# Dense attention's first three steps in a written order, two projection stores on SyncE's queue, softmax maxima apart from stored tiles, and one modulation group moved from layer 0's feed-forward part to layer 1's

## The chip, the cores and the metric

One core of one Trainium2 chip. The metric is device microseconds of one execution; the time of a kernel is the median of its runs.

## The reference, cut to what matters

Two layers (`DEPTH` = 2) over a sequence of 1024 tokens of width 1024. Each layer computes six modulation vectors from the condition c, projects the normed x once for three groups of heads, attends in three ways, projects back, and runs a gated feed-forward part:

```python
for l in range(DEPTH):
    mod = cond @ w_mod[l] + b_mod[l]
    sh_a, sc_a, gt_a, sh_f, sc_f, gt_f = [m[:, None, :] for m in split_cols(mod, (D,) * 6)]
    h = rms_norm(x, g_attn[l]) * (1 + sc_a) + sh_a
    proj = h @ w_in[l]
    ...
    ya = neighborhood_attention(...)        # 4 heads (A)
    yb = sliding_window_attention(...)      # 6 heads (B)
    yc = axial_attention(...)               # 6 heads (C), dense softmax over 1024 keys
    ...
    y = jnp.concatenate([rms_norm(ya, ga), rms_norm(yb, gb), rms_norm(yc, gc)], axis=-1)
    x = x + gt_a * (y @ w_o[l])
    h = rms_norm(x, g_ffn[l]) * (1 + sc_f) + sh_f
    gate, up = split_cols(h @ w_gu[l], (FFN_HIDDEN, FFN_HIDDEN))
    x = x + gt_f * ((jax.nn.silu(gate) * up) @ w_down[l])
return rms_norm(x, g_final)
```

## The kernel before, in words

All matmuls are float32 products made of three matmuls on split operands: an operand is cast to a high part (ACT, `CAST`) and the rest is kept as a low part (DVE, a subtraction). Each layer runs in four stages: the projection, attention, the output projection, and the feed-forward part.

**Who sets the order.** Every engine is wrapped (class `Engine`, lines 36 to 61). Where an engine is pinned (`pin(..., True)`) its instructions keep the order in which the code writes them; where it isn't, a scheduler orders them. Since the wrapper issues every instruction, all of them have line 49 in the profile, and rows are told apart by their tiles.

**The projection's end.** The loop over `oc` (line 1179) projects heads A and B in eight blocks of columns with two halves each (tile `ps_ab`, split into `qko`) and stores each to memory one turn later (`store(act)`, and a last one at line 1203: `qkd<-qko`). In block 7, `early_scores` (line 1161) computes scores, maxima and exponentials of the first two pairs of heads C, whose probabilities lie in `pr` and `wst`. Then pools are closed, and those of attention opened over their space (`y`, `att`), so that a new tile can lie where a stored tile lay and then has to wait until the store has read it.

**Attention** is one stream of 64 pairs of 128-query blocks (`stream`): 24 of heads C (`PairC`, line 1325), 16 of heads A, 24 of heads B. Step n of the loop at line 1587 works on several pairs at once. For heads C it transposes pair n (`turn`: tile `T`, four transposes for four key blocks, cast by ACT and split by DVE to `pt`), multiplies the transposed probabilities of pair n−1 with the values (`pv`), and computes pair n+3's scores (`qk`, which calls `c_scores`, line 1139: four matmuls to a bank of `sC`, of which there are two; DVE's maximum `rs`; ACT's exponential `pr` with its sum). A pair's reciprocals (DVE) and its scaling (POOL) come when both its blocks are done (`divide`, line 1155; `finish` puts them in `unfinished`). Steps with n < 0 only make pairs and their scores. On SP's queue stand, at this place, stores of v for heads A (`vAd<-vs`), tables of biases (`skA`, `skB`), loads of v (`vs<-vAd`) and later the loads of q and k for heads A and B (`qk<-qkd`).

**Modulation in pieces.** A modulation vector of 1024 columns (a group) is an accumulation over 8 blocks of rows of `w_mod`, on DVE (`acc<-wmt,condT,acc`), summed over partitions by four matmuls (`ps_mod`). Some of the groups are computed in steps spread through the projections (`mod_one`), others in the feed-forward part, where the steps are taken from a generator (`mod_stream`): one 512-column half of a block at each `next`, and at a group's end two flushes, each a cast to `acch`, a subtraction to `accl` and the two matmuls that read them. `todo` lists the groups in order; `mod_stream` goes on until a given (layer, group).

**The feed-forward part** computes seven products for each 2x2 block of columns instead of eight (`PRODUCTS`; tile `ps_w`, 12 matmuls each). DVE, POOL and ACT prepare weights (`ws`, `wpt`) and combine products (`u`, `sg`). From block `EARLY` = 7 on, each product is followed by one `next(mods_due, None)`.

Of the kernel before, what the change touches and what calls it, by code (L numbers as in the profile page):

```python
# [19 lines left out]
P = 128  # L20
# [3 lines left out]
H = 512  # L24
# [61 lines left out]
def trunk(ctx: ExitStack, tc, A, C, out):  # L86
# [5 lines left out]
    def pin(engines, on):  # L92
        for e in engines:
            e.pinned = on
# [724 lines left out]
    for l in range(2):  # L819
# [319 lines left out]
        def c_scores(h, j, c, pr, rs):  # L1139

            g = qkC[h // 3]
            s = psS.tile([P, 1024], F32, name="sC", tag="S")
            for kb in range(2):
                ks = slice(kb * 512, (kb + 1) * 512)
                for i in range(2):
                    pe.matmul(
                        s[:, ks], g[:, h % 3, j * P : (j + 1) * P], g[:, 3 + i, ks],
                        start=(i == 0), stop=(i == 1),
                    )
            dve.tensor_reduce(out=rs[:, c : c + 1], in_=s, axis=AX.X, op=ALU.max, negate=True)  # L1150
# [27 lines left out]
        for oc in range(NE, 8):  # L1178
            w = wab
            for half in range(2):  # L1180
# [9 lines left out]
                if store:  # L1190
                    store(act)
                if scored:
# [9 lines left out]
                store = ab_split(oc, half, ps, ab)  # L1202
        store(act)
        pin((pe, act, dve, pool), False)
        close(ab_cm)
# [23 lines left out]
        pad(atp, 16)  # L1229
        gss = {23: gss_tile()}  # L1230
        def pt_tile():
            return wp.tile([P, 4, 256], F32R, name="pt", tag="whl", bufs=8)
# [94 lines left out]
        class PairC(Pair):  # L1327
# [4 lines left out]

            def qk(self, c):
                pr = self.pr[c] = pr_tile()
                c_scores(self.h, 2 * self.p + c, c, pr, self.rs)
                self.finish(pr)

            def turn(self, c):
                if c == 0:
                    self.pt = [[pt_tile() for _ in range(2)] for _ in range(2)]  # L1340
                cc = slice(c * P, (c + 1) * P)
                for kb in range(2):
                    T = t_tile()
                    for i in range(4):
                        kc = kb * 4 + i
                        pe.transpose(T[:, i, :], self.pr[c][:, kc * P : (kc + 1) * P], ident)
                    split_pt(T, self.pt[kb][0][:, :, cc], self.pt[kb][1][:, :, cc])
# [253 lines left out]
        for n in range(-AHEAD - 1, N + 3):  # L1601
            ahead = AHEAD if n + AHEAD < NC else AHEAD_B
            begin = range(done, min(n + ahead + 1, N))
            if n < NC:
                for i in range(2):
                    if 0 <= n:
                        pairs[n].turn(i)
# [12 lines left out]
            else:  # L1620
# [19 lines left out]
                scored, worked = fresh, scored  # L1640
            done = max(done, min(begin.stop, made))
            while made < min(N, n + ahead + 2):
# [3 lines left out]
                made += 1  # L1646
            pin((pe, act, dve), False)
            for what in later.pop(n, []):
# [28 lines left out]
            for end, (chunks, width) in norms.items():  # L1677
                if begins[end] <= m <= end and (m - begins[end]) % 8 == 7 and (n <= NC or m >= NC):
# [9 lines left out]
                    if m == end and end < N - 1:  # L1688
# [335 lines left out]

        mods_due = mod_stream(psl, (ntp, "sq", 2, H), (1, 3))
        bs = []
# [26 lines left out]
        for q in range(NF):  # L2053
# [9 lines left out]
            for i, p in enumerate(PRODUCTS[2 if q < EARLY else 0 :]):  # L2063
# [4 lines left out]
                g_step()  # L2068
                if q >= EARLY:
                    next(mods_due, None)  # L2070
# [331 lines left out]
```

## Time and profile before

| | |
|---|---|
| median of 3 runs | 2403.49 us (2403.01 to 2408.04) |
| profiled execution | 2405.66 us |
| its span | 2403.9 us, at a mean granted TensorE clock of 0.993 |
| TensorE (PE) busy | 2337.2 us (97%) |
| VectorE (DVE) busy | 1756.9 us (73%) |
| ScalarE (ACT) busy | 1192.2 us (50%) |
| GpSimd (POOL) busy | 744.0 us (31%) |

PE is TensorE, PEld its loading of weights, SP is SyncE; a name with a q is an engine's queue of transfers. In a timeline's row stand the start and the duration in us, engine, line, operation, output<-inputs, sizes and the count of instructions drawn together; in brackets the idle time of that engine ahead of it, and whose end ended it. In a row of a stretch stand its length and each engine's busy time with its number of instructions, then the granted clock of PE (1.00 is full speed), the share of the DMA engines' time, and GB/s.

### The profile page before, as it was taken

Reading aid. Unit: us, or ns where it says so; the run is one execution under the profiler, and the core shown is the slowest. Engines: PE = TensorE matmul, PEld = TensorE weight load, DVE = VectorE, ACT = ScalarE, POOL = GpSimd, SP = SyncE. Lnnn points to the kernel's source line nnn. Section 1 sums busy time; section 2 is a strip of 40 time slices with the busy share of each in tenths; the row PEclk is TensorE's granted clock in tenths of the full one; section 3 lists DMA queues with packets and bytes.
Section 4 is the critical chain, followed back from the end, with each engine's and each line's share of the span. In section 5 each row is a group of like instructions: output and inputs, shape, how many; then the busy total and the mean of one; then the engine's idle time right before and its main releaser. Section 6 shows DMA issues by size and latency. Waiting matters only on the chain. (4 is left out here: it accounts for less than half of the span.)

```text
span 2403.9 us, 33342 instructions
## 1 busy us (share of the span) xinstructions
PE 2337.2 (97%) x11733; PEld 1954.9 (81%) x11733; DVE 1756.9 (73%) x2788; ACT 1192.2 (50%) x2250; POOL 744.0 (31%) x719
## 2 busy tenths in 40 slices
PE   8999999999999999999999999999999999999998
PEld 4788899888787887888887879988888888888886
DVE  5767898977858788587677679988797554547765
ACT  3422788944543333344543148897454334334443
POOL 1431345610244443300036114465004443430001
PEclk9999999999999999999999999999999999999999
DMA  8458316154345454586424761152534333329633
GB/s 265 138 183 278 94 62 156 45 201 129 109 137 171 155 186 152 174 265 197 155 88 123 246 215 28 44 145 74 199 103 145 114 101 106 122 88 298 213 125 110
DMA packets 305336, 356.95 MB, mean 148 GB/s; under 512 B 51964, under 2 KB 221788, under 8 KB 305168
## 3 DMA queue, kind: packets, MB, share of 16 engines
q1 hardware_dynamic: 283296, 342.07, 44.9%
q10 hardware_dynamic: 21504, 12.59, 2.0%
q8 instruction: 92, 1.51, 0.3%
q14 instruction: 76, 0.62, 0.1%
q0 software_dynamic: 368, 0.17, 0.0%
HBM read 269.79 MB, written 88.63 MB: 149 GB/s over the span
## 5 line engine op out<-in xcount | busy, mean ns | idle before, releaser
L49 PE MATMUL ps_d<-wpt 128*128 128x512 f32 x1848 | 423.8, 390 | 1.1 <-ACT wpt L49 0.7
L49 PEld LDWEIGHTS ps_d<-wpt 128*128 128x128 f32 x1848 | 345.7, 188 | 74.4 <-issue 3.0
L49 POOL TENSOR_SCALAR pr<-pr,rs 128x1024 f32<-128x1024 f32 (+2 forms) x248 | 193.0, 791 | 220.8 <-DVE rs L49 196.8
L49 POOL TENSOR_TENSOR sg<-sg,u 128x512 f32<-128x512 f32 x82 | 116.6, 1422 | 354.0 <-ACT sg L49 228.4
L49 PE MATMUL pv<-pt,vs 128*128 128x256 f32 x1088 | 175.8, 296 | 17.7 <-DVE y L49 13.4
L49 DVE TENSOR_TENSOR pt<-T,pt 128x512 fp32r<-128x512 f32 x272 | 176.9, 678 | 8.3 <-ACT pt L49 8.0
L49 ACT CAST wpt<-w 128x512 fp32r<-128x512 f32 x154 | 95.7, 621 | 174.6 <-PE ps_d L49 156.1
L49 ACT CAST pt<-T 128x512 fp32r<-128x512 f32 x272 | 151.8, 584 | 40.6 <-PE T L49 38.8
L49 ACT COPY u<-ps_w 128x512 f32<-128x512 f32 x128 | 75.1, 587 | 190.1 <-PE ps_w L49 190.1
L49 POOL TENSOR_TENSOR wpt<-ws,wpt 128x512 fp32r<-128x512 f32 x80 | 110.9, 1388 | 186.5 <-ACT wpt L49 140.3
L49 DVE TENSOR_TENSOR wpt<-w,wpt 128x512 fp32r<-128x512 f32 x154 | 108.9, 707 | 79.8 <-ACT wpt L49 77.7
L49 PEld LDWEIGHTS pv<-pt,vs 128*128 128x128 f32 x1088 | 141.7, 190 | 30.8 <-DVE y L49 26.0
L49 PE MATMUL T<-identr,pr 128*128 128x128 f32 x1176 | 161.6, 273 | 0.8 <-DVE edge L49 0.4
L49 PEld LDWEIGHTS T<-identr,pr 128*128 128x128 f32 x1176 | 137.9, 140 | 16.0 <-issue 1.3
L49 DVE SCALAR_TENSOR_TENSOR acc<-wmt,condT,acc 128x512 f32<-128x512 f32 (+1 forms) x98 | 113.9, 1172 | 44.6 <-DMA wmt<-in_w_mod_dram 44.2
L49 ACT CAST wpt<-ws 128x512 fp32r<-128x512 f32 x176 | 107.8, 622 | 60.0 <-issue 28.1
L49 DVE TENSOR_TENSOR wpt<-ws,wpt 128x512 fp32r<-128x512 f32 x96 | 82.9, 872 | 62.0 <-ACT wpt L49 61.9
L49 DVE TENSOR_TENSOR wpt<-graw,wpt 128x512 fp32r<-128x512 f32 x154 | 110.1, 715 | 17.4 <-ACT wpt L49 17.4
L49 ACT CAST wpt<-graw 128x512 fp32r<-128x512 f32 x154 | 95.0, 617 | 52.9 <-DMA graw<-gpd 48.8
L49 DVE TENSOR_REDUCE rs<-sC 128x1 f32<-128x1024 f32 x88 | 107.3, 1221 | 17.7 <-PE sC L49 12.3
L49 DVE TENSOR_TENSOR ws<-wr 128x512 f32<-128x512 f32 x88 | 78.9, 899 | 53.9 <-POOL wpt L49 50.8
L49 PE MATMUL sC<-qk 128*128 128x512 f32 x384 | 107.5, 403 | 5.8 <-ACT pr L49 5.6
(300 smaller groups left out, 5938.0 us busy)
## 6 DMA issues: line engine op xcount, KB each, us to landing
wr<-in_w_gu_dram SPq DMA_DIRECT2D x92, 512.0 KB, 4.1
gpd<-sg SPq DMA_DIRECT2D x154, 256.0 KB, 4.4
graw<-gpd SPq DMA_DIRECT2D x76, 512.0 KB, 3.5
w<-in_w_down_dram SPq DMA_DIRECT2D x110, 256.0 KB, 5.6
wmt<-in_w_mod_dram SPq DMA_DIRECT2D x48, 512.0 KB, 5.3
qk<-qkd SPq DMA_DIRECT2D x44, 512.0 KB, 7.1
wst<-in_w_o_dram SPq DMA_DIRECT2D x32, 512.0 KB, 4.1
wmt<-in_w_mod_dram SPq DMA_DIRECT2D x64, 256.0 KB, 3.6
```

What stands on the lines that cost most here:

```text
L49: ins = op(*args, **kwargs)
```

## The change

- `c_scores` is split into `c_dots` (the matmuls) and `c_exps` (the maximum and the exponential), so that they can be written apart.
- Steps n < 0 only make pairs. Step 0 is written out, and PE, ACT and DVE stay pinned from the projections through it: the first pair's transposes stand ahead of and between the third's scores, the maxima and exponentials behind the first pair's splits. In step 1 only the fifth pair's scores are computed.
- The stores of the last two halves (block 7, first half: issued one turn later, and the second half) are issued by SP instead of ACT: four transfers in each layer.
- A tile `rb` of the pool `att` is allocated earlier, so that the maxima (`rs`) come to lie elsewhere than on stored tiles.
- In layer 0's feed-forward part three groups are computed instead of four, in layer 1's one instead of none, and `next(mods_due, None)` is left out after two of the seven products.

```diff
@@ projection loop
-                    store(act)
+                    store(sp if oc == 7 and half else act)
...
-        store(act)
-        pin((pe, act, dve, pool), False)
+        store(sp)
+        pin((pool,), False)
...
         gss = {23: gss_tile()}
+        atp.tile([P, H], F32, name="rb", tag="rb", bufs=2)
@@ class PairC
+            def dots(self, c):
+                self.s = c_dots(self.h, 2 * self.p + c)
+                return lambda s=self.s: self.exps(s, c)
+
+            def exps(self, s, c):
+                pr = self.pr[c] = pr_tile()
+                c_exps(s, c, pr, self.rs)
+                self.finish(pr)
...
-            def turn(self, c):
-                if c == 0:
+            def turn(self, c, kbs=(0, 1)):
+                if c == 0 and kbs[0] == 0:
...
-                for kb in range(2):
+                for kb in kbs:
@@ the stream's loop
-            if n < NC:
+            if n < 0:
+                begin = range(done, done)
+            elif n == 0:
+                first, second, third, fourth = (pairs[i] for i in range(4))
+                first.turn(0)
+                exps = [third.dots(0)]
+                first.turn(1)
+                exps.append(third.dots(1))
+                exps[0]()
+                second.turn(0, (0,))
+                first.pv(0)
+                second.turn(0, (1,))
+                first.pv(1)
+                exps[1]()
+                begin = range(3, 4)
                 for i in range(2):
+                    exps = fourth.dots(i)
+                    if i == 0:
+                        second.turn(1)
+                    exps()
+                    while i == 0 and unfinished:
+                        unfinished.pop(0)()
+                done = 4
+                fresh = []
+            elif n < NC:
+                for i in range(2 if n > 1 else 0):
...
+                for i in range(2 if n == 1 else 0):
+                    pairs[begin[0]].qk(i)
...
-            pin((pe, act, dve), False)
+            if n >= 0:
+                pin((pe, act, dve), False)
...
-            pin((pe, act, dve), n >= NC - 1)
+            pin((pe, act, dve), n < 0 or n >= NC - 1)
@@ the feed-forward part
-        mods_due = mod_stream(psl, (ntp, "sq", 2, H), (1, 3))
+        mods_due = mod_stream(psl, (ntp, "sq", 2, H), (1 + l, 2 - 2 * l))
...
-                if q >= EARLY:
+                if q >= EARLY and i % 3 != 2:
                     next(mods_due, None)
```

Three places of the order. First, PE at the start of layer 0's attention, from the projection's last matmul on (`sC` are scores of the third and fourth pairs; `T` from `pr` transposes the first pair, `T` from `wst` the second), before:

```order
L49 MATMUL ps_ab<-hl,whi 128x512
L49 MATMUL sC<-qk 128x512 x8
L49 MATMUL T<-identr,pr 128x128 x12
L49 MATMUL pv<-pt,vs 128x256
L49 MATMUL T<-identr,pr 128x128 x4
L49 MATMUL T<-identr,wst 128x128 x4
L49 MATMUL pv<-pt,vs 128x256 x8
L49 MATMUL sC<-qk 128x512 x4
L49 MATMUL T<-identr,wst 128x128 x6
```

and after:

```order
L49 MATMUL ps_ab<-hl,whi 128x512
L49 MATMUL T<-identr,pr 128x128 x8
L49 MATMUL sC<-qk 128x512 x4
L49 MATMUL T<-identr,pr 128x128 x8
L49 MATMUL sC<-qk 128x512 x4
L49 MATMUL T<-identr,wst 128x128 x4
L49 MATMUL pv<-pt,vs 128x256 x8
L49 MATMUL T<-identr,wst 128x128 x4
L49 MATMUL pv<-pt,vs 128x256 x8
L49 MATMUL sC<-qk 128x512 x4
L49 MATMUL T<-identr,wst 128x128 x8
L49 MATMUL sC<-qk 128x512 x4
```

The first pair's transposes moved ahead of the third pair's scores, and the second's transposes and both blocks of pv stand ahead of the fourth's scores. On DVE at the same place (`qko` is the projection's last split, `pt` the splits of transposed blocks, `rs` the maxima and the reciprocals), before:

```order
L49 SCALAR_TENSOR_TENSOR qko<-ps_ab,qko 128x512
L49 TENSOR_TENSOR pt<-T,pt 128x4x128 x2
L49 TENSOR_REDUCE rs<-sC 128x1 x2
L49 TENSOR_TENSOR pt<-T,pt 128x4x128 x2
L49 TENSOR_REDUCE rs<-sC 128x1
L49 RECIPROCAL rs<-rs 128x2
```

and after:

```order
L49 SCALAR_TENSOR_TENSOR qko<-ps_ab,qko 128x512
L49 TENSOR_TENSOR pt<-T,pt 128x4x128 x4
L49 TENSOR_REDUCE rs<-sC 128x1
L49 TENSOR_TENSOR pt<-T,pt 128x4x128 x2
L49 TENSOR_REDUCE rs<-sC 128x1
L49 TENSOR_TENSOR pt<-T,pt 128x4x128 x2
L49 TENSOR_REDUCE rs<-sC 128x1
L49 RECIPROCAL rs<-rs 128x2
```

Four splits instead of two stand ahead of the first maximum, and two more ahead of the second. Third, PE in layer 0 where heads C end and heads A begin (`sA` are A's scores), before:

```order
L49 MATMUL sC<-qk 128x512 x4
L49 MATMUL T<-identr,pr 128x128 x12
L49 MATMUL sA<-qk 128x256 x2
L49 MATMUL sA<-qk 128x384 x2
L49 MATMUL pv<-pt,vs 128x256 x8
L49 MATMUL T<-identr,pr 128x128 x4
L49 MATMUL pv<-pt,vs 128x256 x8
L49 MATMUL T<-identr,pr 128x128 x8
L49 MATMUL pv<-pt,vs 128x256 x8
```

and after:

```order
L49 MATMUL sC<-qk 128x512 x4
L49 MATMUL T<-identr,pr 128x128 x12
L49 MATMUL pv<-pt,vs 128x256 x8
L49 MATMUL T<-identr,pr 128x128 x4
L49 MATMUL pv<-pt,vs 128x256 x8
L49 MATMUL T<-identr,pr 128x128 x8
L49 MATMUL pv<-pt,vs 128x256 x8
L49 MATMUL T<-identr,pr 128x128 x8
L49 MATMUL pv<-pt,vs 128x256 x6
L49 MATMUL sA<-qk 128x256 x2
L49 MATMUL sA<-qk 128x384 x2
```

The first scores of A stand 30 pv and 20 transposes later. In the feed-forward part of layer 0, PE has 24 `ps_w` matmuls between a group's two flushes in each of four groups before; after the change it has 24, 36 and 36 in three groups, and 24 in layer 1's one.

More of the change, by code (lines that the diff above doesn't have):

```diff
@@ L1139, in c_scores, with c_dots @@
         def c_scores(h, j, c, pr, rs):
+            c_exps(c_dots(h, j), c, pr, rs)
+        def c_dots(h, j):
             g = qkC[h // 3]
@@ L1149, in c_scores, with c_exps @@
                     )
+            return s
+        def c_exps(s, c, pr, rs):
             dve.tensor_reduce(out=rs[:, c : c + 1], in_=s, axis=AX.X, op=ALU.max, negate=True)
@@ L1331, in __init__ @@
                 self.pr = first_pairs.pop(0) if first_pairs else [None, None]
-            def qk(self, c):
-                pr = self.pr[c] = pr_tile()
-                c_scores(self.h, 2 * self.p + c, c, pr, self.rs)
-                self.finish(pr)
-            def turn(self, c):
-                if c == 0:
+            def dots(self, c):
[5 more added lines that the diff above has]
+                self.finish(pr)
+            def qk(self, c):
+                self.dots(c)()
+            def turn(self, c, kbs=(0, 1)):
+                if c == 0 and kbs[0] == 0:
                     self.pt = [[pt_tile() for _ in range(2)] for _ in range(2)]
                 cc = slice(c * P, (c + 1) * P)
-                for kb in range(2):
+                for kb in kbs:
                     T = t_tile()
@@ L1640, in trunk @@
                 scored, worked = fresh, scored
-            done = max(done, min(begin.stop, made))
+            done = max(done, min(begin.stop, made)) if n >= 0 else done
             while made < min(N, n + ahead + 2):
```

## The prediction

> **What bounds the kernel now.** I read the page's first lines, then the busy time in equal stretches, then the waits at the places the change touches, and last the granted clock. First the page:
>
> ```profile
> span 2403.9 us, 33342 instructions
> PE 2337.2 (97%) x11733; PEld 1954.9 (81%) x11733; DVE 1756.9 (73%) x2788; ACT 1192.2 (50%) x2250; POOL 744.0 (31%) x719
> ```
>
> TensorE is idle for only 2403.9 − 2337.2 = 66.7 us. The change leaves the arithmetic alone, so it can only win or lose in those 66.7 us and in stretches at a lower clock. The next view gives, for each stretch, its length and then the busy time of PE, PEld, DVE, ACT and POOL, the granted clock, the DMA share and GB/s.
>
> ```profile
> 240.00:260.00 20.00, 14.92 (x82) 12.34 (x81) 12.03 (x18) 8.46 (x15) 2.39 (x3) 1.00 0.80 238
> 380.00:400.00 20.00, 19.21 (x150) 17.70 (x147) 17.05 (x59) 18.54 (x53) 11.21 (x18) 1.00 0.71 182
> 760.00:800.00 40.00, 37.36 (x157) 30.20 (x156) 32.19 (x41) 13.64 (x25) 16.26 (x12) 0.96 0.42 136
> 1420.00:1440.00 20.00, 16.25 (x97) 13.89 (x97) 14.35 (x21) 13.19 (x25) 6.64 (x6) 0.91 0.47 139
> ```
>
> The first is the start of attention in layer 0 (5.08 us idle), the fourth the same place in layer 1 (3.75, and a mean clock of 0.91), the second the passage from heads C to heads A, the third a flush of a modulation group in layer 0's feed-forward part. These are the four places that the change reaches. At layer 0's start the timeline shows two stalls; the bracket at a row's end is the idle time before it and what ended it:
>
> ```profile
> 246.73 1.98 PE L49 MATMUL sC<-qk 128*128 128x512 f32 x8
> 246.93 0.60 ACT L49 ACTIVATE qko<-ps_ab 128x512 fp32r<-128x512 f32 x1 [0.46 <-PE ps_ab L49]
> 247.56 0.69 DVE L49 SCALAR_TENSOR_TENSOR qko<-ps_ab,qko 128x512 fp32r<-128x512 f32 x1 [0.89 <-ACT qko L49]
> 248.29 2.25 ACTq L49 DMA_DIRECT2D qkd<-qko  x2
> 248.55 1.47 PE L49 MATMUL T<-identr,pr 128*128 128x128 f32 x12
> 250.58 1.57 ACT L49 CAST pt<-T 128x512 fp32r<-128x512 f32 x3 [3.05 <-PE T L49]
> 251.20 1.29 DVE L49 TENSOR_TENSOR pt<-T,pt 128x512 fp32r<-128x512 f32 x2 [2.94 <-ACT pt L49]
> 251.70 0.39 PE L49 MATMUL pv<-pt,vs 128*128 128x256 f32 x1 [1.68 <-ACT pt L49]
> 255.05 2.36 DVE L49 TENSOR_REDUCE rs<-sC 128x1 f32<-128x1024 f32 x2 [2.57 <-DMA qkd<-qko]
> 256.31 1.11 ACT L49 ACTIVATE pr<-sC,rs 128x1024 f32<-128x1024 f32 x1 [3.09 <-DVE rs L49]
> 257.57 1.20 PE L49 MATMUL sC<-qk 128*128 128x512 f32 x4 [3.36 <-ACT pr L49]
> ```
>
> ACT's queue issues the last two stores until 250.54, and only then casts the first transposed block: 1.68 us. DVE's first maximum waits for those stores to land, until 255.05; the exponential waits for it, and PE for the bank that the exponential frees: 3.36 us. Layer 1 has the same two, 1.43 and 2.28:
>
> ```profile
> 1421.63 1.24 ACTq L49 DMA_DIRECT2D qkd<-qko  x2
> 1424.04 0.39 PE L49 MATMUL pv<-pt,vs 128*128 128x256 f32 x1 [1.43 <-ACT pt L49]
> 1426.31 2.36 DVE L49 TENSOR_REDUCE rs<-sC 128x1 f32<-128x1024 f32 x2 [1.49 <-DMA qkd<-qko]
> 1428.83 1.20 PE L49 MATMUL sC<-qk 128*128 128x512 f32 x4 [2.28 <-ACT pr L49]
> ```
>
> Last the clock, in the 3.41 us stretches at whose edges it changes:
>
> ```profile
> 252.45:255.86 3.41, 1.72 (x14) 1.40 (x12) 0.84 (x2) 0.59 (x1) 0.00 (x0) 1.00 0.83 213
> 255.86:259.28 3.42, 1.71 (x11) 1.49 (x12) 3.22 (x5) 2.83 (x6) 0.00 (x0) 1.00 0.96 294
> 774.69:778.10 3.41, 0.90 (x3) 0.19 (x1) 3.41 (x5) 1.10 (x2) 2.48 (x2) 1.00 0.05 18
> 778.10:781.52 3.42, 3.29 (x8) 2.62 (x9) 2.99 (x7) 0.00 (x0) 0.00 (x0) 0.50 0.63 207
> 1426.64:1430.05 3.41, 1.22 (x6) 1.00 (x7) 3.22 (x4) 2.48 (x4) 0.00 (x0) 1.00 0.08 27
> 1430.05:1433.46 3.41, 3.41 (x14) 2.92 (x13) 2.45 (x4) 2.20 (x6) 1.95 (x2) 0.50 0.44 143
> ```
>
> A stretch in which PE was busy for 0.90 or 1.22 us is followed by one at half speed; after 1.72 and 1.71 the clock stays. A stretch at half speed does 1.7 us of work in 3.4, so each such step costs up to **1.7 us**, twice in this kernel behind its start. By the Trainium skill, "TensorE: Matmul & The Clock Gate", section "Why this matters for your kernels", it is gaps of more than about 3 us that drop the clock: this trace disagrees, as 3.36 us in layer 0 (split over two stretches) left it and 2.28 in layer 1 (inside one) halved it. By that rule the sum below would hold no halving and be −5.4 instead of −4.2.
>
> **The change, part by part.** The base is the profiled execution, 2405.66 us (2403.9 of span and 1.8 around it). The sum is a difference; I apply it to the median of the three runs, 2403.49, which lies 2.2 below that execution.
>
> *Attention's start.* Counts stay; the order and two waits change. PE issues one score matmul each (1.98 − 0.39)/7 = 0.23 us, one transpose each 0.11. In layer 0, from 246.73: T x8, scores x4, T x8, scores x4 and T x4 follow with pv x8 between them. ACT, without the stores in its queue, casts as soon as T is there: four casts (1.57 for three, one each 0.5) until about 250.2. DVE splits four blocks (1.29 for two) behind its 247.56 row: until 251.0. Then the first maximum (2.36 for two, 1.2 for one) until 252.2, the first exponential (1.11) until 253.4; two casts and two splits until 255.1, the second maximum until 256.4, the second exponential until 257.6. PE has work that needs none of it until 253.3, waits 0.35 us for the first exponential, transposes until 255.3, and then waits **2.3 us** for the second exponential to free a bank of scores. Behind it four score matmuls and pv x16 last until 260.6; the third pair's blocks come only after the maximum and the reciprocal of DVE (260.6) and POOL's scaling (1.13, as in its row beside): another 1.2, and 1.0 more for the next bank. That is 0.35 + 2.3 + 1.2 + 1.0 = 4.8 us against 1.68 + 3.36 = 5.04: **−0.2** in layer 0. The waits for the stores are gone, but what is late next is DVE: the written order puts four splits ahead of the first maximum. Layer 1 has 1.43 + 2.28 + 1.7 (clock) = 5.4 now and the same 4.8 then: **−0.6**. Whether the 2.3 us fall into one stretch of 3.41 depends on phase: PE's busy share must stay under about a third (1.22) and be safe at a half (1.71); a 2.3 us gap lying wholly within leaves 1.1, which happens for (3.41 − 2.3)/3.41 = 0.33 of phases, and a little more counts the 0.35: 0.4 in each layer. One halving in two layers is the likeliest single count that isn't none (0.48 against 0.36); I take a share of it, since later idle time absorbs some: **+1.2**, with 0 and 3.4 as ends.
>
> *The stores on SP.* They stand on SP ahead of these, which come later by the wait for the split:
>
> ```profile
> 222.34 10.95 SPq L49 DMA_DIRECT2D vAd<-vs  x8
> 254.12 5.22 SPq L49 DMA_DIRECT2D vs<-vAd  x8
> 302.77 1.91 SPq L49 DMA_DIRECT2D qk<-qkd  x3
> ```
>
> The eight stores of vs, skA and skB wait behind them until about 248.3 and move by some 24 us; vs<-vAd with them, from 254 to about 283. The first reader is the load at 302.77, whose heads are computed from 371 us on. The cover is 20 us at the load; without it the delay would meet the first scores of A only 68 us later. I cost it at nothing.
>
> *C to A in layer 0.* The order puts the first scores of A 30 pv and 20 transposes later, though their loads are issued at 302.77 as now. The nearest row is the stretch 380 to 400, idle 0.79 us now. From below, the delay gives nothing or takes those 0.79 away; from above it adds as much as the next stretches show each (1.93 from 440 to 460). I take 0.79 once more: **+0.8**. Layer 1's order is unchanged there.
>
> *The modulation group.* Layer 0 flushes three groups instead of four, and takes 5 steps in 7 products. These rows are PE's stalls there, DVE's cast behind one of them, the waits of the whole feed-forward part (waiter, releaser, us, times), and what waited for the tile acc:
>
> ```profile
> 776.25 0.50 PE L49 MATMUL ps_mod<-acch,onesr 128*128 128x512 f32 x1 [1.16 <-DVE acch L49]
> 778.23 0.79 PE L49 MATMUL ps_mod<-accl,onesr 128*128 128x512 f32 x1 [1.48 <-DVE accl L49]
> 959.97 0.73 PE L49 MATMUL ps_w<-ht2h,wpt 128*128 128x512 f32 x2 [1.40 <-ACT u L49]
> ```
>
> ```profile
> 775.08 1.11 DVE L49 CAST acch<-acc 128x512 fp32r<-128x512 f32 x1
> ```
>
> ```profile
> DVE acc L49 <- DMA wmt<-in_w_mod_dram: 41.5, 25, 5.3
> ```
>
> ```profile
>   PE ps_mod L49: 3.8, 4
> ```
>
> The flushes cost 3.8 us, the wait at 959.97 (ACT behind DVE, which stands behind additions that wait for wmt, 41.5 us in all) 1.40: 5.2 in four groups, 1.3 each, and one halving of 1.7. All this is taken away: **−5.2 −1.7**. What comes back: between a group's two flushes stand 24 matmuls (24 x 0.23 = 5.5 us) in all four groups before; after it 24, 36 and 36 in layer 0, so two groups have 2.8 us more, over the largest stall of 1.48. The first group keeps its 24 and I leave it 1.3. Layer 1 gets a group with 24. Its DVE has room:
>
> ```profile
> 720.00:760.00 40.00, 40.00 (x178) 33.12 (x177) 30.68 (x37) 15.27 (x27) 18.16 (x13) 1.00 0.55 184
> 1900.00:1940.00 40.00, 40.00 (x178) 33.11 (x177) 19.88 (x24) 15.84 (x28) 17.21 (x14) 1.00 0.35 119
> ```
>
> DVE is busy for 19.88 of 40 us in layer 1 against 30.68 in layer 0, so of its ends, 0 and 1.3, I take 0.2. Together **+1.5**, with 0 and 6.9 as ends (all of it back). The group's own matmuls only move.
>
> Sum: −0.2 −0.6 +1.2 +0.8 −5.2 −1.7 +1.5 = **−4.2**; 2403.49 − 4.2 = **2399.3**.
>
> **The rivals.** (a) *The stalls are per group, whatever the pace.* Four groups remain, at 1.3 each, and only the halving goes: −0.2 −0.6 +1.2 +0.8 −1.7 = −0.5, 2403.0. For it: the count of groups is the same, and the wait for wmt is a wait for a load. Against it: half of layer 1's DVE is free. (b) *All of it goes:* no stall at a flush, no halving at the starts, none at C to A: −0.2 −0.6 −6.9 = −7.7, 2395.8. (c) *Slower, through the clock.* The 2.3 us gap falls inside one stretch in both layers (+3.4), and the two flushes with 24 matmuls, in layer 0 and in layer 1, each stall as at 776 (1.16 + 1.48) and halve the clock (+1.7): 2 x 4.3 − 6.9 = +1.7. With −0.2 −0.6 +0.8: +5.1, 2408.6. It decides from a busy time below about 1.2 us of 3.41. For it: both events stand in the trace; against it: four of four must happen. (d) *The maxima wait for the landing all the same,* or for something as late. Then the starts stay as now with layer 1's halving: +0.8 −5.2 −1.7 +1.5 = −4.6, 2398.9. Against it: the order shows no such wait left, so 2398.9 differs from the forecast only because I find little gain in the starts.
>
> **How the numbers follow.** Forecast 0.48, (a) 0.18, (b) 0.15, (c) 0.14, (d) 0.05. A measurement of this kernel can tell about 0.2%, 4.8 us, from no change: faster is below 2398.7, slower above 2408.3. The forecast is split at its own line: without a halving it is at 2398.1, with one at 2399.3 or above, half each. Faster: 0.24 + 0.15 + 0.03 = 0.42; slower: 0.13, nearly all of (c); the rest, 0.45, within. The range runs from 1.8 below (b), for C to A gaining 0.79 and 1.0 more in the starts, to just under (c): 2394.0 to 2408.0.
>
> **What would show it.** Right: no DMA wait before the first maxima; a gap of about 2.3 us before the fourth pair's second block of scores at each start, ended by ACT's exponential; stalls before ps_mod below 1.5 us in all. Wrong: the starts' idle time well under 4 us (then DVE's order hurts less than I count), stalls before ps_mod in layer 1 as large as at 776 us, or PE waiting for qk at 371 us because of the stores on SP.

## The result, and the profile after

The changed kernel takes 2399.27 us (median; 2396.59 to 2401.06), the kernel before 2402.89 us beside it: a ratio of 0.998, 95% interval 0.9973 to 0.9987, so between 3.1 and 6.5 us faster, about 3.6 by the medians. Run again on another chip it was 0.9988 of the kernel before (0.998 to 0.9997). The prediction's 2399.3 is met, but, as the experiments show, by terms that err both ways.

The profiled execution took 2400.17 us. First the page of after:

```profile
span 2398.0 us, 33296 instructions
PE 2339.5 (98%) x11733; PEld 1958.6 (82%) x11733; DVE 1754.4 (73%) x2788; ACT 1191.1 (50%) x2250; POOL 745.5 (31%) x719
```

TensorE's idle time fell from 66.7 to 58.5 us. Its stretches that answer to the four of before (columns as there; layer 1's start now lies some 8 us earlier):

```profile
240.00:260.00 20.00, 17.66 (x103) 14.95 (x102) 13.87 (x22) 9.31 (x17) 2.22 (x2) 0.99 0.53 168
380.00:400.00 20.00, 18.30 (x141) 16.93 (x140) 17.40 (x61) 18.06 (x53) 11.23 (x18) 1.00 0.64 157
760.00:800.00 40.00, 39.66 (x175) 32.44 (x174) 32.05 (x41) 14.53 (x26) 18.44 (x13) 1.00 0.48 156
1412.00:1432.00 20.00, 17.42 (x103) 14.80 (x101) 14.85 (x21) 12.50 (x23) 3.64 (x5) 0.91 0.87 270
```

At the flush the idle time went from 2.64 to 0.34 us; at layer 0's start from 5.08 to 2.34; from C to A it rose from 0.79 to 1.70. The timeline of layer 0's start shows what is late there now:

```profile
251.14 1.22 DVE L49 TENSOR_REDUCE rs<-sC 128x1 f32<-128x1024 f32 x1
252.39 1.12 ACT L49 ACTIVATE pr<-sC,rs 128x1024 f32<-128x1024 f32 x1 [2.00 <-DVE rs L49]
253.65 1.19 PE L49 MATMUL sC<-qk 128*128 128x512 f32 x4 [0.23 <-ACT pr L49]
254.10 1.29 DVE L49 TENSOR_TENSOR pt<-T,pt 128x512 fp32r<-128x512 f32 x2 [1.75 <-ACT pt L49]
255.31 1.21 DVE L49 TENSOR_REDUCE rs<-sC 128x1 f32<-128x1024 f32 x1
256.56 1.11 ACT L49 ACTIVATE pr<-sC,rs 128x1024 f32<-128x1024 f32 x1 [2.00 <-DVE rs L49]
257.82 1.19 PE L49 MATMUL sC<-qk 128*128 128x512 f32 x4 [2.10 <-ACT pr L49]
258.85 3.42 PE L49 MATMUL pv<-pt,vs 128*128 128x256 f32 x16
260.95 2.21 POOL L49 TENSOR_SCALAR pr<-pr,rs 128x1024 f32<-128x1024 f32 x2 [11.82 <-DVE rs L49]
```

No DMA stands in a bracket: the waits for the stores are gone. But the second maximum starts at 255.31, since the written order puts the splits of 254.10 ahead of it, and TensorE waits 2.10 us for the exponential behind it. Layer 1 has the same 2.10 at 1422.04. Both starts are followed by a stretch at half clock, and so are two other places (of the rows below two pairs show both stretches, the last two only the one ahead of the halved one):

```profile
256.02:259.43 3.41, 1.61 (x8) 1.28 (x9) 1.66 (x3) 2.17 (x4) 0.00 (x0) 1.00 0.59 213
259.43:262.84 3.41, 3.41 (x17) 3.25 (x16) 2.45 (x4) 1.74 (x3) 1.89 (x2) 0.50 0.32 114
1276.60:1280.00 3.40, 1.74 (x14) 1.31 (x13) 2.63 (x4) 1.96 (x6) 3.40 (x3) 1.00 0.00 0
1280.00:1283.40 3.40, 3.40 (x9) 2.64 (x8) 3.33 (x7) 0.19 (x1) 3.32 (x4) 0.50 0.50 154
1420.00:1423.40 3.40, 1.36 (x6) 1.02 (x7) 1.65 (x3) 2.17 (x4) 0.00 (x0) 1.00 0.97 326
1607.70:1611.10 3.40, 2.88 (x24) 2.61 (x24) 1.91 (x7) 2.83 (x8) 1.28 (x3) 1.00 0.26 63
```

In the feed-forward part no flush stalls any more. The four rows are both flushes of the first group in layer 0; none has a bracket. The row behind them is DVE's wait for the loaded rows of `w_mod` over the same 300 us as before:

```profile
791.93 0.39 PE L49 MATMUL ps_mod<-acch,onesr 128*128 128x512 f32 x1
792.16 0.39 PE L49 MATMUL ps_mod<-accl,onesr 128*128 128x512 f32 x1
797.87 0.39 PE L49 MATMUL ps_mod<-acch,onesr 128*128 128x512 f32 x1
798.10 0.39 PE L49 MATMUL ps_mod<-accl,onesr 128*128 128x512 f32 x1
```

```profile
DVE acc L49 <- DMA wmt<-in_w_mod_dram: 48.0, 24, 5.1
```

That wait did not shrink with the groups (41.5 us for four, 48.0 for three), and yet the stalls are gone. So it was not what made them.

Most of what follows compares stages of the profiles, since a stage is free of most of what happens elsewhere. Each number is the difference of two starts on TensorE's timeline: *start* from the projection's last matmul to the 65th matmul of heads C's scores behind it; *C to B* from there to the first scores of heads B, in layer 0; *FF 0* from the first `ps_w` to layer 1's first `ps_ab`; *FF 1* from the first `ps_w` to the first `ps_d`. The last column lists where the clock fell to a half behind 100 us and ahead of 2380.

| kernel | start 0 | start 1 | C to B | FF 0 | FF 1 | halvings at |
|---|---|---|---|---|---|---|
| before | 45.57 | 46.09 | 122.60 | 683.33 | 423.75 | 778, 1430 |
| after | 45.66 | 45.60 | 123.89 | 673.18 | 424.95 | 259, 1280, 1423, 1611 |
| after_again | 45.66 | 45.52 | 123.86 | 675.50 | 425.49 | 258, 1422 |
| mods_only | 47.14 | 45.78 | 122.58 | 675.85 | 425.19 | 256, 1420 |
| start_only | 45.35 | 45.49 | 123.87 | 681.14 | 424.41 | 445, 1428, 1616 |
| group_only | 47.81 | 44.23 | 122.60 | 680.49 | 430.63 | 256, 779, 1946 |
| pace_only | 47.82 | 45.41 | 122.60 | 691.57 | 423.50 | 256, 1007 to 1024, 1298, 1441 |
| stores_rb | 42.95 | 42.93 | 124.82 | 682.51 | 423.97 | 777 |
| rb_only | 42.61 | 42.70 | 122.56 | 683.79 | 423.87 | 441, 581, 1612 |
| no_order | 42.95 | 42.93 | 124.82 | 677.83 | 425.99 | 1281, 1609 |
| no_order_pool | 42.97 | 43.03 | 122.60 | 679.67 | 426.40 | 444, 583, 1611 |
| idle_filled | 45.34 | 45.35 | 123.90 | 675.67 | 425.27 | 447, 1284 |
| max_first | 42.85 | 42.85 | 123.74 | 676.02 | 424.92 | none |
| max_first_pool | 44.46 | 43.37 | 122.62 | 674.83 | 424.63 | 264, 1277 |

A row is one profile and holds the halvings that it drew. before, mods_only, group_only and pace_only have the same code at both starts, and yet their first start took 45.57 us without a halving and 47.14 to 47.82 with one, their second 44.23 without and 45.41 to 46.09 with one. So a difference of two rows of about 2 us can be the clock's alone.

### The profile page after: what moved, and what is told of

Its sections match the earlier page's. It is cut to its first block, busy times and chain, and to the rows that moved or that the text cites. A ratio compares the mean times of both kernels' runs of the same rounds, so it can differ in the third digit from the quotient of the medians.

```text
span 2398.0 us, 33296 instructions
## 1 busy us (share of the span) xinstructions
PE 2339.5 (98%) x11733; PEld 1958.6 (82%) x11733; DVE 1754.4 (73%) x2788; ACT 1191.1 (50%) x2250; POOL 745.5 (31%) x719
## 5 line engine op out<-in xcount | busy, mean ns | idle before, releaser
L49 ACT CAST pt<-T 128x512 fp32r<-128x512 f32 x272 | 151.0, 584 | 36.5 <-PE T L49 35.4
```

What stands on the lines that cost most here:

```text
L49: ins = op(*args, **kwargs)
```

## The experiments

Each ratio is that of the kernel's time to the kernel before on the same chip.

**The two halves of the change: mods_only and start_only.** mods_only is the kernel before with this:

```diff
-        mods_due = mod_stream(psl, (ntp, "sq", 2, H), (1, 3))
+        mods_due = mod_stream(psl, (ntp, "sq", 2, H), (1 + l, 2 - 2 * l))
...
-                if q >= EARLY:
+                if q >= EARLY and i % 3 != 2:
```

> The kernel before with only the modulation group moved (three groups in layer 0's feed-forward part at 5 steps in 7 products, one in layer 1's). Theory: this part carries all of the gain and more. Between the two profiles layer 0 from its first to the next layer's first projection matmul went from 683.3 to 673.2 us, layer 1's feed-forward part from 423.5 to 424.7: -10.1 + 1.2 = -8.9, of which a halving of the clock at 778 us is 1.7. So 2402.9 - 7.2 to 8.9 = 2394.0 to 2395.7. Rival: the two profiles differ by chance there and the start of attention gives its share of the gain: then this gives -1.5 to -3.6, about 2400.

Measured: 2398.71 us, 0.998 (0.9971 to 0.9988), so 2.9 to 7.0 us faster. That lies between the theory and its rival: the group alone gives as much as the whole change, but less than the stages said (FF 0 −7.5, FF 1 +1.4). start_only is the changed kernel with those two lines as before.

> The changed kernel with the modulation groups as before: written order, stores on SyncE and the moved maxima alone. Theory: the parts add up, and the start of attention is worth nothing or costs: what the group alone gains beyond the 3.6 us of the whole change is lost here, +3 to +5 us with both starts at half clock (1.7 us each) and C to A later by about 1.3; 2405 to 2408. Rival, the written order helps: the stalls of layer 0's start went from 5.0 to 2.3 us, so -2.5 in each layer, 2398.

Measured: 2405.63 us, 1.0005 (0.9995 to 1.0015), so between 1.2 us faster and 3.6 slower: no difference that can be told. A gain of 5 us is excluded, a loss of 3 isn't, though the median lies only 0.8 above. The written order, the stores on SyncE and the moved maxima are together worth nothing that shows: the stages say −0.2 and −0.6 at the starts and +1.3 from C to B.

**The group without its pace: group_only.** The kernel before with the first of the two edits only.

> The kernel before with the groups divided between the layers, but a step taken after every product as before (so 24 matmuls between all flushes). Theory of the pace: the stalls come from flushes that follow too closely, so at most the share of the one group that leaves layer 0 is gained, a quarter of 5.2 us: -1.3, and layer 1's group may stall too: 2401 to 2403. Rival, number alone: what matters is that layer 0 has one group less to load and add, whatever the pace: most of the gain of the version with the pace, within 1.5 us of it.

Measured: 2408.41 us, 1.0018 (1.0009 to 1.0027): slower by 2.2 to 6.5 us. Both expectations are wrong. The group computed in layer 1 stalls there, though VectorE has more room, and by more than any group of layer 0; the timeline of its two flushes:

```profile
1936.53 0.39 PE L49 MATMUL ps_mod<-acch,onesr 128*128 128x512 f32 x1
1936.76 0.39 PE L49 MATMUL ps_mod<-accl,onesr 128*128 128x512 f32 x1
1944.45 0.50 PE L49 MATMUL ps_mod<-acch,onesr 128*128 128x512 f32 x1 [1.82 <-DVE acch L49]
1946.13 0.80 PE L49 MATMUL ps_mod<-accl,onesr 128*128 128x512 f32 x1 [1.18 <-DVE accl L49]
```

VectorE's rows just ahead show why the cast for the second flush is late:

```profile
1933.40 1.66 DVE L49 TENSOR_TENSOR accl<-acc,acch 128x512 fp32r<-128x512 f32 x1
1934.99 1.77 DVE L49 TENSOR_TENSOR wpt<-ws,wpt 128x512 fp32r<-128x512 f32 x1
1936.85 1.62 DVE L49 TENSOR_TENSOR ws<-wr 128x512 f32<-128x512 f32 x1
1938.51 1.66 DVE L49 TENSOR_TENSOR ws<-ws,wr 128x512 f32<-128x512 f32 x1
...
1942.09 0.68 DVE L49 TENSOR_TENSOR u<-u,ps_w 128x512 f32<-128x512 f32 x1
1942.68 0.68 DVE L49 TENSOR_TENSOR acc<-ps_mod,identr 128x512 f32<-128x512 f32 x1
1943.29 1.11 DVE L49 CAST acch<-acc 128x512 fp32r<-128x512 f32 x1
```

Between the flushes VectorE has the weights of a product to prepare, three rows of them at 1.6 to 1.8 us, and only then the row `u` of a product that TensorE had finished, the sum of the first flush and the cast. These three rows stand beside three of GpSimd that follow one behind the other:

```profile
1934.72 1.49 POOL L49 TENSOR_TENSOR u<-u 128x512 f32<-128x512 f32 x1 [0.21 <-ACT u L49]
1936.29 1.64 POOL L49 TENSOR_TENSOR sg<-sg,u 128x512 f32<-128x512 f32 x1
1937.87 1.75 POOL L49 TENSOR_TENSOR wpt<-wr,wpt 128x512 fp32r<-128x512 f32 x1
```

In the profile of before all 237 of VectorE's TENSOR_TENSOR rows that make `ws` or `wpt` out of `wr` and `ws` and that no row of GpSimd overlaps take 0.68 or 0.69 us; of the 89 that one overlaps, 73 take more than 1 us. What the stalls of all profiles have in common is not the distance of the two flushes but their place among the seven products. Second flushes between the products on h11 and h21, with the first behind the one on h22, stall in every profile that has them, among these before, start_only and group_only (1.32 + 1.76, 1.35 + 1.73, 1.33 + 1.75 in layer 0, 1.98 + 1.45 in layer 1, as excess over 0.23 us from start to start). First flushes ahead of the product on h11 and second ones behind the one on h21, also 24 matmuls apart, stall in none: at 834 and 840 of before, at 792 and 798 of after, at 1956 and 1962 of after in layer 1. Between 834 and 838 GpSimd has no row in before, and VectorE's rows for `ws` and `wpt` take 0.68 us each. A third place, 895 and 902 of before, stalls for less (0.65 + 0.97). Leaving out two steps in seven moves the first group's flushes from one kind of place to the other. No run moves the place alone: each pair that stalls most is the first group of its feed-forward part, and the second and third groups of after have 36 matmuls between their flushes as well as other places.

**The pace without the group: pace_only.** The kernel before with the second edit only.

> The kernel before with only the pace changed: steps after 5 of 7 products, all four groups still in layer 0. Theory (the pace, not the count, removes the stalls at the flushes): no wait of over 1 us before ps_mod in the feed-forward part, so -4 to -6 as with the groups moved too; but a group takes 22 steps, four take 88, and 5 in 7 of the 105 products behind the seventh block are 75: 13 steps are left to the end and run one behind the other. If they lie beside the down projection, about 2399 on the scale of 2403 to 2405 for the kernel before; if they are waited for, some 13 x 2 us of loads and additions are not hidden, and this is slower than before by 5 or more. Rival (the count matters): the stalls stay, 2403 to 2405.

Measured: 2418.38 us, 1.0059 (1.0047 to 1.0072): slower by 11 to 17 us, the case of the expectation in which the rest is waited for. The first three groups' flushes stall nowhere; the fourth's stand at the end of the loop, between `ps_w` and the down projection, and there the clock is at a half for 17 us:

```profile
1011.46 0.79 PE L49 MATMUL ps_mod<-acch,onesr 128*128 128x512 f32 x1 [6.95 <-DVE acch L49]
1014.56 0.79 PE L49 MATMUL ps_mod<-accl,onesr 128*128 128x512 f32 x1 [2.31 <-DVE accl L49]
1016.58 0.77 PE L49 MATMUL ps_mod<-acch,onesr 128*128 128x512 f32 x1 [1.22 <-DVE acch L49]
```

So the two edits need each other: the pace puts the flushes where they don't stall, and at that pace four groups don't fit into layer 0.

**The start: stores_rb, rb_only, no_order.** stores_rb is the kernel before with

```diff
-                    store(act)
+                    store(sp if oc == 7 and half else act)
...
-        store(act)
+        store(sp)
...
         gss = {23: gss_tile()}
+        atp.tile([P, H], F32, name="rb", tag="rb", bufs=2)
```

> The kernel before with the two stores on SyncE and the maxima moved, but no written order. Theory (the waits for ScalarE's queue and the landing are what costs at the start, the order only says what is next): no stall of 3.36 and 1.68 us there; the first maximum at about 251 instead of 255, the next stall a wait for an exponential of 1 to 2 us; -1 to -3 for each start, but the first scores of heads A come later in layer 0 by over 5 us as in the changed kernel, +1.3. Sum -1 to -4. Rival (the stall is VectorE's own work behind the casts, so another wait takes the place of the one removed): within 1 us of the kernel before.

Measured: 2401.64 us, 0.9989 (0.998 to 0.9998), −3.8 by the medians: the theory's size, and the starts give −2.6 and −3.2, where the whole change gives +0.1 and −0.5. rb_only has only the last of the three lines.

> The kernel before with only the maxima moved; the stores stay on ScalarE's queue. Theory: the second stall (3.36 and 2.28 us, the landing of the store) shrinks to 1 us as in the version with both, the first (1.68 and 1.43, ScalarE's queue) stays; C to A unchanged, since nothing moves on SyncE: -2 to -3 in both layers together, and the halving at 1430 us may go (-1.7): 2400 to 2402 where the kernel before is at 2404.8. Rival (the stores on ScalarE delay the casts so far that the maxima behind them come as late as with the wait): within 1 us of the kernel before.

Measured: 2399.80 us, 0.9983 (0.9974 to 0.9993), −4.7 by the medians, the good end of what was expected: the one allocated tile gives all of the gain at the starts, −3.0 and −3.4, and C to B is unchanged. Of the −3.4 in layer 1 only 1.6 are waits (3.71 us idle before, 2.13 here); the rest is the halving at 1430 that before drew, and against group_only's second start, without one, the gain is 1.5. Its timeline:

```profile
249.13 0.39 PE L49 MATMUL pv<-pt,vs 128*128 128x256 f32 x1 [1.37 <-ACT pt L49]
249.37 0.66 PE L49 MATMUL T<-identr,pr 128*128 128x128 f32 x4
250.06 0.63 PE L49 MATMUL T<-identr,wst 128*128 128x128 f32 x4
250.44 1.19 PE L49 MATMUL pv<-pt,vs 128*128 128x256 f32 x8
252.33 1.20 PE L49 MATMUL sC<-qk 128*128 128x512 f32 x4 [0.70 <-ACT pr L49]
```

The stall behind ScalarE's queue stays (1.37 us, 1.68 before), as expected; the other fell from 3.36 to 0.70. Taking the stores off ScalarE's queue removes the first as well, but stores_rb waits for splits and exponentials instead, and its start is no shorter (42.95 against 42.61). no_order is the changed kernel without its written order, that is stores_rb with the groups moved.

> The changed kernel without its written order: the stores on SyncE, the maxima moved and the groups moved, but step 0 and the steps before it as in the kernel before. Theory (the waits removed are worth about 2.7 us at each start, and the written order gives that away again): from the last projection matmul to the third pair's heads in layer 0 and 1 the profile takes 42.9 us instead of 45.6, so 2 x 2.7 less than the changed kernel, but about 0.9 more at C to A in layer 0, since A's first scores stand later still (384 transposes and 368 pv instead of 368 and 350): -4.5 against the changed kernel, 2395 to 2396.5. Rival (the difference between the starts is made up later in the stage): within 1 us of the changed kernel.

Measured: 2397.44 us, 0.9971 (0.996 to 0.9982), where the changed kernel on the same chip was at 2400.99: −3.6 by the medians, near the theory's −4.5. By the stages the written order costs 2.7 us in each layer, of which up to 0.3 is the halved clock (see idle_filled).

**The place of heads A's scores: no_order_pool and max_first_pool.** Both put the stores on GpSimd's queue (`store(pool if oc == 7 and half else act)` and `store(pool)`).

> As no_order, with the two stores issued by GpSimd instead of SyncE, which puts A's first scores back to where they stood before the change. Theory (the later place in the order, and nothing that SyncE does on the chip, costs 1.1 to 2.2 us at C to A): from C's last scores to B's first it takes 122.6 us as in the kernel before, not 124.8, so 1.5 to 2.2 less than no_order: 2393.5 to 2394.5. Rival (the version with the maxima first gained only 0.1 us in the median from this, so it is given back elsewhere): within 0.7 us of no_order.

Measured: 2396.78 us, 0.997 (0.996 to 0.9981), 0.7 us less than no_order: by the time alone inconclusive. The stage decides: C to B takes 122.60 again instead of 124.82. What the stores moved was only the order that was laid down for TensorE, in which A's first scores came 30 to 48 pv later; SyncE's own rows in the changed kernel show the loads for A where they were (302.77 before), long ahead of the first scores at 378:

```profile
265.21 9.14 SPq L49 DMA_DIRECT2D vs<-vAd  x8
303.01 1.91 SPq L49 DMA_DIRECT2D qk<-qkd  x3
```

In this stage TensorE is idle for 3.15 us in after and 1.64 in before, with new waits for VectorE (0.60 at 372) and GpSimd (0.61 at 391); why the later place brings them isn't shown. Layer 1's passage, whose order is unchanged, takes 122.56 to 122.62 in every profile.

**VectorE's written order: max_first.** The changed kernel with its step 0 written so (the maximum and the exponential of a block can be called apart):

```diff
-                exps = [third.dots(0)]
+                max0, exp0 = third.dots(0)
+                max0()
                 first.turn(1)
-                exps.append(third.dots(1))
-                exps[0]()
+                max1, exp1 = third.dots(1)
+                max1()
+                exp0()
                 second.turn(0, (0,))
                 first.pv(0)
+                exp1()
                 second.turn(0, (1,))
                 first.pv(1)
-                exps[1]()
...
-                    exps = fourth.dots(i)
+                    most, exps = fourth.dots(i)
+                    while unfinished:
+                        unfinished.pop(0)()
                     if i == 0:
                         second.turn(1)
+                    most()
                     exps()
-                    while i == 0 and unfinished:
-                        unfinished.pop(0)()
```

> The changed kernel with the first step's order written otherwise: each of the third pair's maxima stands on VectorE right behind the splits of the block before it instead of behind two more, the exponentials behind the casts that are ready, and the third pair's division ahead of the second pair's last transposes. Theory (VectorE's written order is what leaves 2.10 us idle at each start, and the halved clock follows from it): first maximum at 249.6 instead of 251.1, second exponential's end at 254.4 instead of 257.6, so that the fourth pair's second scores wait for nothing; instead about 0.5 us ahead of the first pair's values. Worth 0.23 + 2.10 - 0.5 = 1.8 in each layer and 1.7 for each halving gone: -3.6 to -7.0 against the changed kernel, 2392 to 2396. Rival (the work must be done by VectorE anyhow and the wait only moves behind it): within 1 us of the changed kernel, 2399.

Measured: 2394.54 us (2393.07 to 2396.47), 0.996 (0.9948 to 0.9973), as the theory had it: 2.8 us less in each start, and no halving. On its timeline 0.18 us are left of the stalls of the first step and 1.61 us come later:

```profile
250.34 1.10 PE L49 MATMUL pv<-pt,vs 128*128 128x256 f32 x7 [0.18 <-DVE pt L49]
...
254.38 1.17 PE L49 MATMUL sC<-qk 128*128 128x512 f32 x4
...
262.94 1.19 PE L49 MATMUL sC<-qk 128*128 128x512 f32 x4 [1.61 <-ACT pr L49]
```

This is faster than both kernels. With the stores on GpSimd:

> The version with the maxima first, with the two stores issued by GpSimd instead of SyncE. In its order the first scores of heads A stand where they stood before the change (348 transposes and 320 pv matmuls behind the projection, instead of 375 and 352), so this tells what the later place cost. Theory (the later place of A's scores costs layer 0 about 1.2 us from C's last scores to B's first): -1.2 against the version with the maxima first, 2393. Rival one (that place costs nothing, the difference is in how the steps overlap): within 0.5 us. Rival two (GpSimd's issue delays its scaling of the second pair): a stall before the second pair's transposes of over 1 us at each start, +2.

Measured: 2394.43 us, 0.9958 (0.9946 to 0.9971), the same time as max_first, as its first rival had it; in its profile C to B is 1.1 us shorter, as the theory had it, and a halving at 264 us behind the same wait of 1.6 us takes the start from 42.85 to 44.46. Which of the two is better in the mean stays open.

**The price of a halved clock: idle_filled, after_again.** idle_filled has nine matmuls more in the wait of each start:

```diff
+                    if i == 0:
+                        T = t_tile().rearrange("p a b -> p (a b)")
+                        for _ in range(9):
+                            pe.matmul(
+                                T, qkC[0][:, 0, 0:P], qkC[0][:, 3, 0:512],
+                                start=True, stop=True,
+                            )
```

> The changed kernel with nine more matmuls of 128x512 that nobody reads, put into the 2.10 us in which TensorE waits for the second exponential at each start (work added, none left out). Theory (the idle stretch halves the clock, and that costs up to 1.7 us each): at both starts the clock stays at 1.00, TensorE still takes up the next scores at the same place, and the time falls by 1.5 to 3.4 against the changed kernel although 4 us of matmuls were added: 2396 to 2398 where that is at 2399. Rival (the halvings fall into waits that come anyhow, such as the 1.2 us for the third pair's scaling): no gain, within 0.7 us of the changed kernel.

Measured: 2400.43 us, 0.9979 (0.997 to 0.9988), against 0.998 and 0.9988 of the changed kernel: no gain that can be told. The clock stayed at 1.00 at both starts, as the theory had it, and yet they took 45.34 and 45.35 us instead of 45.66 and 45.60: the rival's cover.

```profile
255.03 2.30 PE L49 MATMUL T<-qk 128*128 128x512 f32 x9
257.37 1.21 PE L49 MATMUL sC<-qk 128*128 128x512 f32 x4
258.42 2.20 PE L49 MATMUL pv<-pt,vs 128*128 128x256 f32 x16
261.69 0.44 PE L49 MATMUL T<-identr,pr 128*128 128x128 f32 x2 [1.07 <-POOL pr L49]
```

At full speed the sixteen pv are done in 2.20 us instead of 3.42, and TensorE then waits 1.07 us for GpSimd's scaling; at half speed it had no such wait. start_only shows the same without added work: its first start drew no halving, took 45.35 us and has that wait with 1.05 us.

> The changed kernel again, for times on the same chip as the other runs of this call: 0.998 of the kernel before, so 2399 to 2400.5 where that is at 2404 to 2405.5. The phase of the clock's stretches differs from execution to execution, so the profile may show a halving at other places than the first did; the time from the last projection matmul to the third pair of heads stays at 45.6 to 45.7 us in layer 0 and 1 whether it is halved there or not, if the halving is covered by the wait for the third pair's scaling; rival: 1.7 us less where there is no halving.

Measured: 2400.99 us, 0.9988 (0.998 to 0.9997). Its clock fell at both starts again and not at 1280 and 1611; the starts took 45.66 and 45.52, so the rival's 1.7 us less without a halving are not there.

## Why the prediction was right, point by point

- **Attention's start: right, row by row.** 4.8 us of stalls in layer 0 for 5.0 before was the forecast, from four waits; start_only's first start, not halved, has all four, 0.23 + 2.10 + 1.05 + 0.72 = 4.10. In after they are 3.05 and 3.15, since the halved clock fills the third. Idle time well under 4 us was named as a sign that VectorE's order hurts less than counted; here it is the half clock that covers the rest. The first maximum at 251.0, the waits of 0.35 and 2.3 us and the end of the second exponential at 257.6 came at 251.14, as 0.23 and 2.10 us, and at 257.7. By stages the starts moved by +0.1 and −0.5 us; the forecast was −0.2 and −0.6. Against the mean of the four profiles with the old starts (47.1 and 45.4) they moved by −1.4 and +0.2, so single profiles agree this well in part by luck. Its reason stands too: the order puts four splits ahead of the first maximum. max_first, which puts the maxima ahead of those splits (and moves exponentials and the third pair's division with them), gains 2.8 us in each start, and no_order, without any written order, 2.7.
- **The halved clock: wrong in its size.** I charged +1.2 for one halving in two starts. Both were halved in both profiles of the changed kernel, one of two in start_only, and idle_filled and start_only show what it costs there: 0.1 to 0.3 us each. The step that failed is that I counted the halving and the wait of 1.2 us for the third pair's scaling side by side; the one fills the other. Also wrong was that a busy time of 1.71 us of 3.41 is safe: 1.61 and 1.74 were followed by half speed in after, and so was 2.88 at 1611. In that last stretch stand 13 matmuls of a single column (`ps_st`, 1.36 of the 2.88 us), and 1.72 kept the clock where 1.74 lost it, so busy time by the records isn't what the gate counts; what it counts, these runs don't show.
- **The stores on SyncE, hidden: right in that no load was late, wrong in what followed.** Their cost comes through the order (C to A).
- **C to A: right in direction, too small.** +0.8 was forecast, +1.3 measured (122.60 to 123.89), and stores on GpSimd give it back whole. I had charged it to the order as such; what puts A's scores later is the stores' move to SyncE.
- **The group: right in sign and, over all profiles, in size, for a reason that is in part wrong.** I forecast −5.2 −1.7 +1.5 = −5.4 and matmuls that only move. FF 0 went down by 10.2 and 7.8 us in the two profiles of the changed kernel, FF 1 up by 1.2 and 1.7. These are good draws: over the eight profiles with both edits FF 0 takes 673.2 to 679.7 us, over the four with neither 681.1 to 683.8, and between the means lie −6.6 in FF 0 and +1.4 in FF 1, −5.3 together. What varies is mainly TensorE's waits for ScalarE at places that are not flushes, near 977 and 1000 us: 0.73 and 0.60 in after_again, 1.13 and 1.29 in no_order_pool, neither in after. In the two profiles, taking the group's four matmuls of 0.23 us (0.9) off on one side and on the other, stalls and halving fell by 9.2 and 6.9 in layer 0 and rose by 0.3 and 0.8 in layer 1, where I had −5.6 and +0.2. The term that failed is "the first group keeps its 24 and I leave it 1.3": that group doesn't stall at all, and a distance of 24 matmuls stalls or not by its place among the products. So does the argument from VectorE's room in layer 1: group_only moved the group there at the old pace, and it stalled for more than any group of layer 0: VectorE's long rows there stand beside GpSimd's, which its mean load doesn't tell. Rival (a), in which every group brings its stall whatever the pace, falls with the flushes of after.
- **The sum.** −4.2 was forecast, −3.6 measured by the medians (−4.8 by the ratio). In the two profiles of the changed kernel the group gave more than I counted, over all eight as much; the halved starts cost less than I charged, and A's place and halvings at other places (1280 and 1611 in the first profile, neither in the second) took more. That the total came within 0.1 us of the forecast is chance to this extent. It also isn't the sum of the profiles' stages: the profiled execution of before lay 2.8 us above its median, that of after 0.9.

## What to carry to other kernels

When a wait is removed by moving data and an order is written in the same step, measure each alone: here one allocation took 3.0 and 1.6 us of waits out of the two starts, and with the order written around it the starts were 2.7 us longer again. Order an engine's queue by who waits longest: a maximum that starts a chain of three engines goes ahead of splits that nobody waits for yet. Work slipped in between products can stall by where it falls in their cycle, not only by how far apart it is; look at what the other engines do there, and try its phase before its amount.

## What the runs showed of the hardware that was not expected

- A halving of TensorE's clock costs little where the next wait is as long as what it loses: 0.3 us at these starts, where without it 1.07 us of waiting for GpSimd come instead. Elsewhere it cost nearly its full size: with the halving at 264 us in max_first_pool the start took 44.46 us instead of 42.85, and the start of the kernel before took 47.14 to 47.82 instead of 45.57.
- VectorE's rows that make `ws` or `wpt` out of `wr` and `ws` take 0.68 or 0.69 us where GpSimd has no row beside them and up to 1.79 where it has one (237 and 89 rows of before). Its rows that take a product from `ps_w` stay at 0.67 to 0.69 beside GpSimd too (36 rows).
- The gate's edges lie 3.41 us apart, but their phase differs between executions: the first fall to half behind 30 us comes at 51.2 us in after and at 36.5 in after_again, two executions of one kernel (51.1 in before, 38.0 in mods_only, 36.6 in max_first). The Trainium skill, "TensorE: Matmul & The Clock Gate", section "What's actually happening", says of the window that it is free-running and isn't reset by a kernel's start; these profiles agree. So one profile shows one draw: after was halved at four places behind 100 us and the same kernel again at two.
- VectorE waited longer for the loads of `w_mod` in the faster kernel (48.0 us for three groups) than in the slower (41.5 for four): idle time ahead of an instruction, even 48 us of it, says nothing on whether anyone waits for that instruction.
